# A hybrid decoder layer on one core: more steps between the attention's loads, rotation and parts, and one between store and load of the recurrence's inverses

## The chip, the core and the metric

The kernel runs on one core of a Trainium2 chip. The metric is the device time of one execution in microseconds; the median of several runs is given. The engines are named as in the profile: PE (TensorE; PEld is its weight load), DVE (VectorE), ACT (ScalarE), POOL (GpSimd) and SP (SyncE, which only issues DMAs here). Each engine works off its own queue in order.

## What is computed

One layer on 2048 tokens of width 1024, with 16 learned meta tokens ahead of them. Two mixers run side by side on one input projection, and a gated feed-forward follows:

```python
u = rms_norm(h, norm_mix_g)
proj = u @ w_in + b_in                       # attention | RWKV | two gates
q, k = partial_rope(q, pos), partial_rope(k, pos)
y_attn = sliding_window_sink_attention(q, k, v, sinks)   # window 128, 8 heads, 2 kv heads
y_rwkv = rwkv7_time_mix(p_rwkv, ...)                     # delta-rule recurrence, 8 heads of 64
merged = gates[..., :D] * (y_attn @ w_br_attn) + gates[..., D:] * (y_rwkv @ w_br_rwkv)
h = h + merged @ w_o
f = rms_norm(h, norm_ffn_g)
h = h + (silu(f @ w_gate) * (f @ w_up)) @ w_down
return rms_norm(h, norm_final_g)[:, 16:]
```

## The kernel before

The dense work goes over four blocks of 512 tokens, in two phases: `phase_a(b)` makes the input projection of block b in 37 chunks of 128 columns (`pi`, eight groups of three matmuls each), for b = 0 to 3; then `phase_c(b)` merges the branches (`pb`, `ph_o`), and does the feed-forward (`pg`, `pu`, `ph_d`), for b = 0 to 3. Projections go to DRAM (`proj_d`), the mixers' outputs too (`y_d`), and phase c of a block loads that block's `y_d` (`yl`, split into `ya`).

The mixers are generators that are ticked between the dense matmuls. A `yield` ends a step. Each dense group of three matmuls yields a credit of 0.65, and for each 4.0 / 3 of credit `tick` runs one of three turns; an attention unit moves on in every third turn, so by one step for each 4 of credit, some six dense groups. The recurrence's units (`rwkv(i, j)`, 33 of them, one for each pair of heads and 256 tokens) move in the other two turns, each by one step per three turns, and a new one starts 14 steps after the youngest. Attention units (`attn(ti)`, 16 of 128 tokens each) follow one another: when the last step of one is done, the next starts in the same turn. All the mixers' matmuls stand in TensorE's queue between the dense ones in the order in which the program writes them (`InOrder`). On the other engines a scheduler with a timeline of its own places the instructions, the dense work's with a higher priority.

One attention unit: loads of `cs`, `q`, `qr` (the rotated halves), `kl`, `kr`, `vt`; a step; rotation on GpSimd (L945 to L947, and `roped`, L894 to L896); `set_keys` (`kw`, L884 and L885: each a rounded part and its rest); `parts(0)` (the query's rounded part `qs`, L955 on ScalarE, and its rest, L956 on VectorE); two steps; then for each of two key heads the scores `psS`, the softmax, and the products `py`. After the last `py` ScalarE copies it into `q` (L1014), whose tile has one buffer, and stores it into `y_d` (L1015).

One unit of the recurrence solves 16 triangular blocks on GpSimd (L772 and L774), waits `WAIT_INV` steps, stores the inverses (`xt_d`, L799), loads them again in another layout into the one tile `td` (L804), a step, transposes them on VectorE (L808), a step, `pq` on TensorE, a step, and then four rounds of three steps with the `ch` matmuls, one of which reads `td`. Three more steps, and `pyt` transposes the unit's output, which goes through L869 to L871 into `y_d` (L872).

Of the kernel before, what the change touches and what calls it, by code (L numbers as in the profile page):

```python
# [78 lines left out]
def layer(ctx, tc, x, meta, w_in, w_br, w_o, w_gate, w_up, w_down, w2a, a2, g2, vecs, sinks, gfin,  # L79
# [38 lines left out]
    def f32(ap):  # L118
        return ap.bitcast(F32)
# [497 lines left out]
    def rwkv(i, j):  # L617
# [179 lines left out]
        for _ in range(WAIT_INV):  # L797
            yield
        G.dma_start(xt_d[uid].rearrange("m (b c) i -> b m (c i)", c=4), xv.rearrange("p c i -> p (c i)"))  # L799
        lo, hi = [slice(64 * h, 64 * h + 32) for h in range(2)], [slice(64 * h + 32, 64 * h + 64) for h in range(2)]  # L800
        for h in range(2):
            for q, r32 in ((0, lo[h]), (1, hi[h])):
# [77 lines left out]
    def set_keys(k, cols):  # L880
        for g in range(2):
            gb = slice(64 * g, 64 * g + 64)
            for d in (gb, slice(64 - 64 * g, 128 - 64 * g)):
                A.activation(kw[d, g, 0, cols], k[gb], AF.Copy)  # L884
                V.tensor_sub(kw[d, g, 1, cols], k[gb], f32(kw[gb, g, 0, cols]))  # L885
# [6 lines left out]
    def roped(o, src, rot, cs, w, name):  # L892

        G.tensor_mul(src, src, cs[:, 0])  # L894
        G.tensor_mul(rot, rot, cs[:, 1])
        G.tensor_add(o, src, rot)  # L896
# [28 lines left out]
    def attn(ti):  # L925
# [14 lines left out]
        load_rot(kr, 4, 1, c0, P)  # L940
        vt = mx.tile([P, P], F32, tag="vl", bufs=1, name=f"vl_{ti}")
        S.dma_start(vt, proj_d[5][:, c0:c0 + P])
        yield
        b4 = lambda k: cs[:, k].unsqueeze(1).to_broadcast([P, 4, P])
        G.tensor_mul(q, q, b4(0))  # L945
        G.tensor_mul(qr, qr, b4(1))
        G.tensor_add(q, q, qr)  # L947
        roped(kl[:, 0], kl[:, 0], kr[:, 0], cs, P, ti)
        set_keys(kl[:, 0], own)

        def parts(g):
# [75 lines left out]
    def tick():  # L1027

        turn[0] = (turn[0] + 1) % TURNS
        rs = [u for u in units if u[2] == "r"]  # L1030
        for u in list(units):
            if turn[0] != (0 if u[2] == "a" else 1 if len(rs) > 1 and u is rs[0] else 2):
                continue
            u[1] += 1
            if next(u[0], 0) == 0:
                units.remove(u)
        if todo_r and turn[0] == 2:
            i, j = todo_r[0]
            b = (i or 0) // 2
            young = min((u[1] for u in units if u[2] == "r"), default=LAG)  # L1040
            if young >= LAG - 3 and i not in asked and set(range(6, 9)) <= emitted[b]:
                asked.add(i)
                start("l", lora(i), b)
            if young >= LAG and i in loras and set(
                    range(9, 21) if i is None else range(PAIR0 + 3 * j, PAIR0 + 3 * j + 3)) <= emitted[b]:
                todo_r.pop(0)
                start("r", rwkv(i, j), b)
        if todo_a and turn[0] == 0 and not any(u[2] == "a" for u in units):
            ti = todo_a[0]
            b = (ti or 0) // 4  # L1050
            if set(range(6)) <= emitted[b]:
                todo_a.pop(0)
                start("a", attn_meta() if ti is None else attn(ti), b)
# [135 lines left out]
```

## Time and profile before

| | |
|---|---|
| median of 3 runs | 3375.84 us (3372.03 to 3376.8) |
| profiled execution, its own time | 3377.94 us |
| its span, first to last instruction | 3376.0 us |
| mean granted TensorE clock | 0.987 of full speed |
| busy: PE / PEld / DVE / ACT / POOL | 96% / 79% / 46% / 34% / 34% |
| first and last score matmul `psS` | 142.6 and 1692.0 us |

The span is what the rows below tell of; the execution's own time has 1.9 us around it. Busy shares are means over stages with different limits, so the waits say more than they do. A row of waits reads: who waited, for whom, us in total, times, longest. A row of the timeline reads: start, length, engine, line, what it writes and reads; in brackets how long its engine stood idle before it and who ended that.

### The profile page before, as it was taken

The page shows a single profiled execution, that of the slowest core. Times are in us where ns is not written, and L with a number is a line of the kernel's source. Part 1 is how long each engine was busy: PE and PEld are TensorE (multiplying, and loading weights), DVE is VectorE, ACT ScalarE, POOL GpSimd, SP SyncE. Part 2 cuts the span into 40 slices and gives each one's busy share as a digit, 9 for nine tenths or more (in the row PEclk, how much of TensorE's full clock was granted, in tenths as well). Part 3 has the DMA queues.
Part 4 walks back from the last instruction along what each step waited for, and adds up shares of the span by engine and source line. Part 5 has one row for each costly group of instructions (what it writes and reads, how often), then busy time and mean ns, then how long its engine had stood idle before and what let it go on. Part 6 is the DMA issues. An engine that isn't in the chain of part 4 may idle for free.

```text
span 3376.0 us, 47237 instructions
## 1 busy us (share of the span) xinstructions
PE 3256.3 (96%) x16909; PEld 2681.2 (79%) x16909; DVE 1542.1 (46%) x3622; ACT 1163.2 (34%) x2863; POOL 1156.1 (34%) x2771
## 2 busy tenths in 40 slices
PE   7899999999999998999999999999999999999998
PEld 6777887787888777887787788887888888778887
DVE  3343233232332585666666644445654443542233
ACT  4354344443443455445443422233242221220001
POOL 1124434334344454554453433444333341000000
PEclk9999999999999999999999999999999999999999
DMA  7777666676666776666668555556755555855555
GB/s 262 273 261 241 209 226 211 190 227 197 223 210 215 242 260 206 234 235 234 231 237 280 176 170 174 179 181 201 263 171 177 171 177 176 288 179 191 196 191 181
DMA packets 229448, 721.46 MB, mean 214 GB/s; under 512 B 36333, under 2 KB 90989, under 8 KB 168286
## 3 DMA queue, kind: packets, MB, share of 16 engines
q1 hardware_dynamic: 158126, 516.15, 47.1%
q0 software_dynamic: 38736, 154.99, 12.9%
q10 hardware_dynamic: 32352, 47.31, 3.8%
q8 instruction: 133, 2.18, 0.3%
q14 instruction: 101, 0.83, 0.1%
HBM read 533.46 MB, written 184.82 MB: 213 GB/s over the span
## 4 chain that ended last, share of the span: by engine, by line
PE 60%; DMA 6%; DVE 3%; POOL 3%; ACT 2%; issue 2%; SPq 0%; POOLq 0%; DVEq 0%; ACTq 0%
PE pg L93 14%; PE pu L93 12%; PE ph_d L93 11%; PE pi L93 6%; PE pb L93 4%; PE ch L93 4%; PE ph_o L93 3%; DMA yl<-y_d 1%; PE ph_o_l L93 1%; POOL pr L772 1%; POOL xv L774 1%; DMA lt<-lt_d 1%; PE py L93 1%; PE pq L93 1%; DVE h L202 1%
## 5 line engine op out<-in xcount | busy, mean ns | idle before, releaser
L93 PE MATMUL pi<-act_u,w_in 128*128 128x512 f32 x3552 | 902.5, 402 | 10.5 <-DVE m L202 6.1
L93 PEld LDWEIGHTS pi<-act_u,w_in 128*128 128x128 f32 x3552 | 652.9, 191 | 144.0 <-issue 5.5
L93 PE MATMUL pg<-act_f,w_g 128*128 128x512 f32 x2112 | 533.7, 399 | 6.8 <-DVE act_f L202 6.8
L93 PE MATMUL pu<-act_f,w_u 128*128 128x512 f32 x2112 | 522.9, 395 | 0.0
L93 PE MATMUL ph_d<-w_d,mg_g 128*128 128x512 f32 x1920 | 472.5, 397 | 10.4 <-DVE h L202 10.0
L93 PEld LDWEIGHTS pg<-act_f,w_g 128*128 128x128 f32 x2112 | 388.4, 189 | 85.3 <-DVE act_f L202 9.0
L93 PEld LDWEIGHTS pu<-act_f,w_u 128*128 128x128 f32 x2112 | 388.9, 188 | 78.8 <-issue 1.0
L93 PEld LDWEIGHTS ph_d<-w_d,mg_g 128*128 128x128 f32 x1920 | 355.5, 189 | 85.9 <-DVE h L202 14.5
L772 POOL TENSOR_TENSOR pr<-xv,lt 128x124 f32<-128x124 f32 (+30 forms) x992 | 330.5, 333 | 248.9 <-DMA lt<-lt_d 176.8
L774 POOL TENSOR_TENSOR xv<-xv,pr 128x124 f32<-128x124 f32 (+30 forms) x992 | 341.1, 344 | 74.5
L202 DVE SCALAR_TENSOR_TENSOR h<-ph_d,h 128x512 f32<-128x512 f32 x320 | 218.9, 689 | 130.0 <-PE ph_d L93 128.3
L93 PE MATMUL pb<-ya,w_br 128*128 128x512 f32 x768 | 191.0, 400 | 1.0 <-DMA w_br<-wd_br 0.6
L93 PEld LDWEIGHTS pb<-ya,w_br 128*128 128x128 f32 x768 | 143.1, 191 | 30.9 <-DVE mg_m L202 1.0
L202 DVE SCALAR_TENSOR_TENSOR th<-th,pg 128x512 f32<-128x512 f32 x88 | 60.4, 687 | 214.6 <-ACT th L202 214.5
L93 PE MATMUL ph_o<-w_o,mg_m 128*128 128x512 f32 x576 | 144.2, 400 | 6.8 <-DVE h L202 3.8
L804 POOL DMA_DIRECT2D td<-xt_d x132 | 72.6, 557 | 225.4 <-PE ch L93 197.3
L202 ACT ACTIVATE th<-pg 128x512 f32<-128x512 f32 x88 | 52.6, 598 | 281.4 <-PE pg L93 281.0
L202 DVE TENSOR_TENSOR th<-th,pu 128x512 f32<-128x512 f32 x88 | 60.5, 687 | 183.8 <-PE pu L93 183.3
L243 POOL TENSOR_TENSOR ss_o<-ss_o,mhalf 128x1 f32<-128x1 f32 x16 | 9.4, 590 | 372.5 <-DVE ss_o L202 372.3
L755 POOL DMA_DIRECT2D lt_d<-g x128 | 71.2, 561 | 184.0 <-DVE g L750 182.0
L202 ACT ACTIVATE mg_g<-th 128x512 fp32r<-128x512 f32 x88 | 55.3, 628 | 222.6 <-DVE th L202 222.5
L93 PEld LDWEIGHTS ph_o<-w_o,mg_m 128*128 128x128 f32 x576 | 106.5, 190 | 31.3 <-DVE h L202 5.2
(356 smaller groups left out, 4512.1 us busy)
## 6 DMA issues: line engine op xcount, KB each, us to landing
w_in<-wd_in SPq DMA_DIRECT2D x111, 1024.0 KB, 5.5
w_g<-wd_g SPq DMA_DIRECT2D x66, 1024.0 KB, 5.0
w_u<-wd_u SPq DMA_DIRECT2D x66, 1024.0 KB, 5.0
w_d<-wd_d SPq DMA_DIRECT2D x60, 1024.0 KB, 5.0
wd_in<-w_in POOLq DMA_DIRECT2D x37, 1024.0 KB, 5.8
w_br<-wd_br SPq DMA_DIRECT2D x24, 1024.0 KB, 7.0
wd_g<-w_g POOLq DMA_DIRECT2D x22, 1024.0 KB, 5.2
wd_u<-w_u POOLq DMA_DIRECT2D x22, 1024.0 KB, 5.3
```

Of the source, the lines that this page charges most:

```text
L93: r = f(*p, **k)
L202: return f(*p, **k)
L243: G.tensor_tensor(ss[:rows, 3:4], ss[:rows, 2:3], mhalf[:rows, 0:1], op=ALU.pow)
L755: G.dma_start(lt_d[uid, m0:m0 + n].rearrange("c j i -> j c i"), g[r32, :, 0, o])
L772: G.tensor_mul(pr[:, :, :n_], xv[:, :, r:r + 1].to_broadcast([P, 4, n_]), lt[:, r, r + 1:].unsqueeze(1).to_broadcast([P, 4, n_]))
L774: G.tensor_add(xv[:, :, r + 1:], xv[:, :, r + 1:], pr[:, :, :n_])
L804: G.dma_start(td[r32, :, r32], xt_d[uid, m0:m0 + 4].rearrange("m j i -> j m i"))
```

## The change

Three places get more `yield`s: one after the store of the inverses, one more between the attention's loads and its rotation, and two between the rotation and `set_keys`. An attention unit has three steps more, a unit of the recurrence one more. No other line changes; lines behind these move by 1 to 4.

```diff
@@ -797,6 +797,7 @@
         for _ in range(WAIT_INV):
             yield
         G.dma_start(xt_d[uid].rearrange("m (b c) i -> b m (c i)", c=4), xv.rearrange("p c i -> p (c i)"))
+        yield
         lo, hi = [slice(64 * h, 64 * h + 32) for h in range(2)], [slice(64 * h + 32, 64 * h + 64) for h in range(2)]
         for h in range(2):
             for q, r32 in ((0, lo[h]), (1, hi[h])):
@@ -940,12 +941,15 @@
         load_rot(kr, 4, 1, c0, P)
         vt = mx.tile([P, P], F32, tag="vl", bufs=1, name=f"vl_{ti}")
         S.dma_start(vt, proj_d[5][:, c0:c0 + P])
-        yield
+        for _ in range(2):
+            yield
         b4 = lambda k: cs[:, k].unsqueeze(1).to_broadcast([P, 4, P])
         G.tensor_mul(q, q, b4(0))
         G.tensor_mul(qr, qr, b4(1))
         G.tensor_add(q, q, qr)
         roped(kl[:, 0], kl[:, 0], kr[:, 0], cs, P, ti)
+        for _ in range(2):
+            yield
         set_keys(kl[:, 0], own)
 
         def parts(g):
```

TensorE's queue between attention units 5 and 6: the last `py_5` with the dense product after it, and the first `psS_6`. `pi_2_16` is the projection's chunk 16 in block 2, in the order of the queue 17, 18 and so on follow; a row with x3 is one dense group. Before:

```order
L93 MATMUL py_5_6420<-ptm_5_1_6688,vm_t_129 128x512
L93 MATMUL pi_2_16_6728<-act_u2_7_5697,w_in_2_16_6726 128x512 x3
L93 MATMUL pi_2_17_6813<-act_u2_0_5560,w_in_2_17_6811 128x512 x3
...
L93 MATMUL pi_2_18_6882<-act_u2_7_5697,w_in_2_18_6880 128x512 x3
L93 MATMUL pi_2_19_7059<-act_u2_0_5560,w_in_2_19_7057 128x512 x3
L93 MATMUL pv_6_7063<-cst_80,vl_6_6803 128x128
L93 MATMUL psS_6_0_0_7069<-kw_126,qs_6_0_6865 128x272 x2
```

And now:

```order
L93 MATMUL py_5_7223<-ptm_5_1_7642,vm_t_129 128x512
L93 MATMUL pi_2_30_7707<-act_u2_5_5568,w_in_2_30_7705 128x512 x3
L93 MATMUL pi_2_30_7707<-act_u2_6_5579,w_in_2_30_7705 128x512 x3
...
L93 MATMUL pi_2_35_7958<-act_u2_0_5439,w_in_2_35_7956 128x512 x3
L93 MATMUL pi_2_35_7958<-act_u2_1_5452,w_in_2_35_7956 128x512 x3
L93 MATMUL pv_6_7965<-cst_80,vl_6_7758 128x128
L93 MATMUL psS_6_0_0_7971<-kw_126,qs_6_0_7889 128x272 x2
```

Between the two stand 18 dense groups before and 37 now; both pieces have moved to later chunks, since units 0 to 5 have three steps more each.

GpSimd's queue behind the solve of the recurrence's unit 1_0, where a rotation follows (unit 6's before, unit 5's now; `kr` and `kl` are the keys, `q` the queries). Before:

```order
L774 TENSOR_TENSOR xv_1_0_6163<-xv_1_0_6163,pr_1_0_30_6255 128x4
L799 DMA xt_d_79<-xv_1_0_6163 8x16x128
L768 DMA xv_1_1_6929<-in_consts 128x128
L804 DMA td_118<-xt_d_79 32x4x32 x4
L895 TENSOR_TENSOR kr_6_6797<-kr_6_6797,cs_6_6787 128x128
L896 TENSOR_TENSOR kl_6_6796<-kl_6_6796,kr_6_6797 128x128
L861 TENSOR_TENSOR gst_0_3_6817<-gst_0_3_6817,mhalf_92 128x4
L945 TENSOR_TENSOR q_6_6789<-q_6_6789,cs_6_6787 128x512
L947 TENSOR_TENSOR q_6_6789<-q_6_6789,qr_6_6790 128x512
```

And now:

```order
L774 TENSOR_TENSOR xv_1_0_6012<-xv_1_0_6012,pr_1_0_30_6104 128x4
L799 DMA xt_d_79<-xv_1_0_6012 8x16x128
L768 DMA xv_1_1_6750<-in_consts 128x128
L896 TENSOR_TENSOR kr_5_6558<-kr_5_6558,cs_5_6548 128x128
L897 TENSOR_TENSOR kl_5_6557<-kl_5_6557,kr_5_6558 128x128
L947 TENSOR_TENSOR q_5_6550<-q_5_6550,cs_5_6548 128x512
L949 TENSOR_TENSOR q_5_6550<-q_5_6550,qr_5_6551 128x512
L805 DMA td_118<-xt_d_79 32x4x32 x4
```

The loads of `td` stand behind the rotation here, no longer ahead of it, and the rotation comes right after the store.

TensorE's queue at the end of phase c of block 2, where the last unit of the recurrence transposes its output (`pyt_7_3`); 15 dense groups stand between `pyt_7_3` and block 3's first `pb_3_0_0` before. Before:

```order
L93 MATMUL ph_d2_l_0_0_28174<-w_d2_l_0_28172,mg_g2_20_28022 128x512 x3
L93 MATMUL pyt_7_3_28178<-cst_80,yt_7_3_27733 128x128 x2
L93 MATMUL ph_d2_l_0_0_28174<-w_d2_l_0_28172,mg_g2_21_28099 128x512 x3
L93 MATMUL ph_d2_l_0_1_28195<-w_d2_l_1_28193,mg_g2_20_28022 128x512 x3
L93 MATMUL ph_d2_l_0_1_28195<-w_d2_l_1_28193,mg_g2_21_28099 128x512 x3
L93 MATMUL ph_d2_l_1_0_28213<-w_d2_l_0_28172,mg_g2_20_28022 128x512 x3
```

And now:

```order
L93 MATMUL ph_d2_l_0_1_28187<-w_d2_l_1_28185,mg_g2_20_28014 128x512 x3
L93 MATMUL ph_d2_l_0_1_28187<-w_d2_l_1_28185,mg_g2_21_28089 128x512 x3
L93 MATMUL ph_d2_l_1_0_28205<-w_d2_l_0_28172,mg_g2_20_28014 128x512 x3
L93 MATMUL ph_d2_l_1_0_28205<-w_d2_l_0_28172,mg_g2_21_28089 128x512 x3
L93 MATMUL ph_d2_l_1_1_28216<-w_d2_l_1_28185,mg_g2_20_28014 128x512 x3
L93 MATMUL pyt_7_3_28220<-cst_80,yt_7_3_27754 128x128 x2
```

`pyt_7_3` has moved back by six dense groups; nine are left between it and block 3.

## Rows read from the trace of the kernel before

**Rows 1.** The page: busy us, share, instructions; the clock in 40 slices.

```profile
PE 3256.3 (96%) x16909; PEld 2681.2 (79%) x16909; DVE 1542.1 (46%) x3622; ACT 1163.2 (34%) x2863; POOL 1156.1 (34%) x2771
...
PEclk9999999999999999999999999999999999999999
```

**Rows 2.** Waits of TensorE, whole span: total us, times, longest.

```profile
PE psS L93 <- DVE qs L956: 27.3, 9, 5.8
...
PE ph_d L93 <- DVE h L202: 10.0, 7, 4.5
...
PE pq L93 <- DVE tq L808: 6.9, 2, 5.2
```

**Rows 3.** Groups by line, the scores: busy, mean ns, idle before, releasers.

```profile
L93 PE MATMUL psS<-kw,qs 128*128 128x272 f32 (+1 forms) x256 | 53.2, 332 | 36.1 <-DVE qs L956 27.3 <-ACT kw L884 7.1 <-ACT sig L674 0.9
```

**Rows 4.** Timeline, all engines, 612 to 639 us: one wait of the scores.

```profile
615.12 0.60 ACT L1014 ACTIVATE q<-py 128x512 f32<-128x512 f32 x1 [2.14 <-PE py L93]
...
618.45 0.37 SPq L935 DMA_DIRECT2D q<-proj_d  x1
...
623.45 1.55 POOL L945 TENSOR_TENSOR q<-q,cs 128x512 f32<-128x512 f32 x1 [13.21 <-DMA q<-proj_d]
...
630.13 0.62 ACT L955 ACTIVATE qs<-q 64x512 fp32r<-64x512 f32 x1
...
633.64 0.30 DVE L808 STREAM_TRANSPOSE tq<-td 32x128 f32<-32x128 f32 x1 [3.40 <-DMA td<-xt_d]
...
636.31 0.69 DVE L956 TENSOR_TENSOR qs<-q,qs 64x512 fp32r<-64x512 f32 x1
...
637.05 1.27 PE L93 MATMUL psS<-kw,qs 128*128 128x272 f32 x4 [5.79 <-DVE qs L956]
```

**Rows 5.** Windows at half clock behind score waits, 1 of 7, and their sum.

```profile
634.70:641.50 6.80, 4.45 (x12) 3.71 (x13) 4.41 (x17) 0.00 (x0) 2.30 (x2) 0.50 0.40 147
...
sum 37.40, PE 26.35 PEld 22.56 DVE 16.63 ACT 10.35 POOL 17.64; mean PE 3.76 PEld 3.22 DVE 2.38 ACT 1.48 POOL 2.52
```

**Rows 6.** Windows at half clock behind `ph_d` and `pq` waits: first, sum of 4.

```profile
1542.60:1546.10 3.50, 3.30 (x9) 2.64 (x10) 3.50 (x8) 0.33 (x1) 3.50 (x6) 0.51 0.70 274
...
sum 17.30, PE 15.20 PEld 12.18 DVE 13.54 ACT 2.23 POOL 6.07; mean PE 3.80 PEld 3.05 DVE 3.39 ACT 0.56 POOL 1.52
```

**Rows 7.** Waits of the other engines, whole span.

```profile
POOL td L804 <- PE ch L93: 197.3, 25, 17.7
...
POOL q L945 <- DMA q<-proj_d: 54.9, 8, 13.2
ACT qs L955 <- POOL q L947: 53.0, 13, 10.9
...
DVE qs L956 <- ACT qs L955: 51.7, 10, 12.9
```

**Rows 8.** Timeline, 1536 to 1543 us: a hold on VectorE reaches TensorE.

```profile
1537.92 0.69 DVE L956 TENSOR_TENSOR qs<-q,qs 64x512 fp32r<-64x512 f32 x1 [4.91 <-ACT qs L955]
...
1542.80 0.80 PE L93 MATMUL ph_d<-w_d,mg_g 128*128 128x512 f32 x1 [4.52 <-DVE h L202]
```

**Rows 9.** Timeline, 2894 to 2937 us: last recurrence unit, start of block 3's phase c.

```profile
2895.10 0.38 PE L93 MATMUL pyt<-cst,yt 128*128 128x128 f32 x2
...
2897.79 0.61 POOL L872 DMA_DIRECT2D y_d<-tl  x1 [14.18 <-DVE tl L871]
...
2906.03 0.63 ACT L202 ACTIVATE ya<-yl 128x512 fp32r<-128x512 f32 x1 [4.10 <-DMA yl<-y_d]
...
2906.69 0.69 DVE L202 TENSOR_TENSOR ya<-yl,ya 128x512 fp32r<-128x512 f32 x1 [2.97 <-ACT ya L202]
...
2908.79 8.44 PE L93 MATMUL pb<-ya,w_br 128*128 128x512 f32 x36 [0.36 <-DVE h L202]
...
2936.74 0.50 PE L93 MATMUL ph_o<-w_o,mg_m 128*128 128x512 f32 x1 [3.33 <-DVE h L202]
```

**Rows 10.** Waits of TensorE, 1230 to 1292 us: first merge and normalisation.

```profile
PE ph_o L93 <- DVE mt L202: 3.1, 2, 2.8
```

## The prediction

> **What bounds the kernel now.** I read the busy shares first [rows 1]: TensorE's matmul row is busy 3256.3 of 3376.0 us and no other engine comes near, so the time is TensorE's own work plus the stretches in which it stands still (about 120 us) plus what a lowered clock costs. The clock row shows nines throughout; the mean granted clock is 0.987. Only edits that change TensorE's waits can move the time, so the next view is who ended them [rows 2]. The attention's score product `psS` waits on the second half of its split queries (`qs`, L956), longest 5.8 us; with its other releasers, among them one wait of 7.1 us on the keys `kw`, the score product stands for 36.1 us [rows 3]. The other causes near the change are `ph_d` waiting for VectorE to empty its PSUM tile (10.0) and the inverse's `pq` (6.9).
>
> Next, one such wait in order of time [rows 4]. The last product `py` of one attention unit ends, ScalarE copies it out of PSUM at 615.12 into `q`, and a store sends it away. Since `q` has one buffer, the next unit's load of `q` is issued only at 618.45; GpSimd, idle 13.21 us for it, starts the rotation at 623.45; ScalarE's half of the split follows at 630.13; VectorE's half runs at 636.31, behind a transpose (L808) that waited 3.40 us for a DMA. `psS` starts at 637.05 after 5.79 us of standing. So the chain took 21.9 us from 615.12, and TensorE had 16.1 us of other work to cover it (637.05 - 5.79 - 615.12).
>
> **Added: three steps in front of the score product.** TensorE runs in program order, so the cover can be counted in its rows: between the last `py` of a unit and the first `psS` of the next stand 18 or 19 dense groups of three matmuls before, and 36 or 37 after (31 in the last unit), in all 15 pairs of units. The first fence shows one pair: three products on before, five on after. A group costs 3 x 8.44 / 36 = 0.70 us [rows 9], so 19 more groups are 13.3 us of added cover, mixer work not counted; 12 more, in the last unit, are 8.4 us. The longest wait is 7.1 us. Nor does the chain slip by the same amount: in the order of after, ScalarE's `qs` row still stands about one product behind `py`, as before, because the scheduler places it when its own timeline has the data, and GpSimd's rotation still follows the inverse's store closely (second fence). All these waits should go; I leave 2 us for a late queue: **-34** (bounds -36.1, and -18 if half the units still wait).
>
> **The clock behind these waits.** [...] With the waits go the falls; I take **-12.5** (bounds -13.2 and -6). [...]
>
> **Added: one step between store and load of the inverses.** What the loads of `td` (L804) wait for is mostly not the store: of 33 units 25 wait for the matmul `ch` that last reads `td`, 197.3 us in all on GpSimd [rows 7]. That matmul, the loads, the transpose and `pq` all move by the same step, so the chain to `pq` is neither longer nor better covered. The two `pq` waits, 6.9 us together [rows 2], are thus not what the step is long for; a step later they fall beside other work of VectorE, and I count half of them gone: **-3** (bounds 0, and -12 with the half-clock work that follows them, all but the first row's of [rows 6]).
>
> **The end of the mixers.** The same step moves the last unit's `pyt` six groups later (third fence), 6 x 0.70 = 4.2 us. The last store of `y_d` waits for it and block 3's last `ya` for that store: today `pyt` at 2895.10, store at 2897.79, split ready at 2907.38, while its user, the fourth group of the product that starts at 2908.79, comes at 2910.9 [rows 9]. Cover of 3.5 us is gone and 0.7 us open; the chain now passes more rows of VectorE and GpSimd. The later 3.33 us wait of `ph_o`, on the load of `h`, may absorb some. **+2** (bounds -0.6 and +5).
>
> **Attention that lasts longer.** 16 units of three more steps run past the end of block 0's second phase: `py_15` stood before that block's successor began and stands 324 rows behind it now. At the normalisation that had attention beside it the merge's product waited 3.1 us for VectorE [rows 10]; I charge the second one the same, **+3** (0 to +7). The added steps put no instruction on any engine, and block 1 needs only units 4 to 7, done over a thousand rows earlier.
>
> **Not priced: holds on other engines.** ScalarE idles 53.0 us at `qs` for the rotation and VectorE 51.7 us behind it [rows 7]. These rows keep their places, so the holds stay. One of them reached TensorE: VectorE, 4.91 us in wait at L956, emptied `ph_d` late, and TensorE stood 4.52 us [rows 8]. All `ph_d` waits together are 10.0 us [rows 2], and such ones can vanish or come anew; I take 0 (bounds -10 and +10).
>
> Sum: -34 - 12.5 - 3 + 2 + 3 = **-44.5**. The profiled execution took 3377.94 us (span 3376.0 and 1.9 around it), so 3333.4; it lies 2.1 above the median of the three runs, so I predict **3331 us** against 3375.84.
>
> **Rivals.** (1) The wait survives in part: in the order of after, the loads of `td` stand shortly ahead of the rotation in units 3, 10 and 12, and they can hold GpSimd up to 17.7 us [rows 7]. 21.9 + 17.7 = 39.6 us against a cover of 16.1 + 13.3 = 29.4 leaves 10.2 us, with 2 for the clock, in three units: +36, so 3367. For it: such a hold sat inside the wait shown. Against: the 21.9 already contain a wait of GpSimd, and the longest hold never met the rotation.
>
> (2) The holds move, and it gets slower: TensorE, no longer stopped at `psS`, arrives earlier at dense tiles that VectorE has not emptied. In the input projection three tiles of 24 matmuls cover that (3 x 24 x 0.234 = 16.8 us, over the longest hold, 12.9); in the feed-forward the `ph_d` tiles have 6 matmuls each, 4.2 us for three. Seven units (9 to 15) run there after the change. The one seen cost 4.52 + 1.65 (half of the 3.30 us that TensorE worked at half clock, [rows 6]) = 6.2 us. It decides at 44.5 / 7 = 6.4 us a unit: near that the time is unchanged, 3376; at 9 us it is 63 us against the 44.5, 3331 + 63 = 3394. Against: six units ran there before too, and [rows 2] give `ph_d` 10.0 us in all.
>
> (3) The second part does what it says after all: the transposes stop waiting for `td`, VectorE holds nothing else up, and the `pq` and `ph_d` waits go with their clock, 15.2 / 2 = 7.6 us [rows 6]. 6.9 + 10.0 + 7.6 less the 3 already counted is 21.5: 3310. Against: the 25 waits for `ch` above.
>
> **How the numbers follow.** Forecast, 3316 to 3356: 0.65. Rival 1, to 3369: 0.13. Rival 3, below 3316: 0.05. Rival 2 near its point: 0.10, above it: 0.07. A difference under 0.2% (6.8 us) is about what measurement of this kernel cannot tell from none. Faster 0.83, same 0.10, slower 0.07. The range 3308 to 3366 leaves out most of rival 2 and the end of rival 1.
>
> **What would show it.** `psS` at most 5 us in TensorE's waits; a mean clock of about 0.990 or more; VectorE's and ScalarE's waits at `qs` still near 50 us; the last `psS` past 1850 us instead of 1692; GpSimd's `td` waits on `ch` near 200 us; one wait of a few us at the start of the last block. The prediction is wrong if `psS` still stands for over 15 us, or if `ph_d`, `h` or `pg` gain what it loses.

## The result and the profile after

The changed kernel takes 3340.09 us in the median of three runs (3336.55 to 3347.81) against 3375.84: 0.9898 of the time before, 95% interval 0.9873 to 0.9923. A second series gave 0.9897 (0.9875 to 0.9919). So it gains 1.0%, some 35 us, of the 44.5 that were predicted; the median lies 9 us above the forecast and inside its range.

The profiled execution of after took 3347.81 us, span 3346.0. Of the profile's page, the busy times and the clock in 40 slices, as in [rows 1]:

```profile
PE 3248.2 (97%) x16909; PEld 2677.9 (80%) x16909; DVE 1554.7 (46%) x3622; ACT 1165.7 (35%) x2863; POOL 1158.7 (35%) x2771
...
PEclk9999999999999999999999999999999999999999
```

Span less busy time is how long TensorE stood: 119.7 us before, 97.8 now, 21.9 less. The busy time itself fell by 8.1 us with the same 16909 matmuls, while the time at half clock, told below, fell too; I put it down to the clock. Together they are the 30.0 us of the two spans. The group of the scores, which in [rows 3] had 36.1 us of idle time before it:

```profile
L93 PE MATMUL psS<-kw,qs 128*128 128x272 f32 (+1 forms) x256 | 51.6, 323 | 4.9 <-ACT vz L968 4.9
```

One wait is left, and it is for neither the queries nor the keys. The last `psS` starts at 1931.6 us, past the 1850 that were forecast, and the mean clock is 0.989 (0.991 in the two other runs). TensorE's waits over the whole span (total us, times, longest), as in [rows 2]:

```profile
PE ch L93 <- ACT rd L836: 7.0, 5, 2.6
PE ph_d L93 <- DVE h L202: 6.9, 7, 2.1
...
PE psS L93 <- ACT vz L968: 4.9, 1, 4.9
PE ph_d_l L93 <- DVE h L202: 4.8, 4, 3.1
PE ch L93 <- ACT yt L848: 4.5, 4, 3.3
PE pp L93 <- ACT sig L674: 4.3, 2, 2.9
...
PE pb L93 <- ACT ya L202: 4.2, 1, 4.2
...
PE ch L93 <- DVE ud L841: 3.6, 2, 3.2
...
PE pq L93 <- DVE tq L809: 2.7, 2, 1.4
```

`psS` has lost 31.2 us, `pq` 4.2 and `ph_d` 3.1. Against that the recurrence's product `ch`, which stood 3.7 us before, all of it behind `yt`, stands 15.1 (7.0 + 4.5 + 3.6), and `pp`, which had no wait, 4.3. These two give back 15.7 us, half of what `psS` gave up. The same view of the other engines, answering to [rows 7], and VectorE's wait at the transposes of `td`, which was 19.2 us in 13 waits:

```profile
POOL td L805 <- PE ch L93: 325.3, 27, 27.5
...
ACT qs L959 <- POOL q L949: 47.3, 13, 8.4
...
DVE qs L960 <- ACT qs L959: 44.0, 12, 10.8
POOL q L947 <- DMA q<-proj_d: 42.7, 6, 12.2
```

```profile
DVE tq L809 <- DMA td<-xt_d: 2.6, 5, 1.0
```

ScalarE and VectorE stand at `qs` nearly as long as before, as forecast. But GpSimd stands at the loads of `td` 128 us longer, and VectorE no longer waits for them, which was not.

The windows in which the granted clock was 0.50 or 0.51 of full speed, called half clock here; columns: window, length, then busy time of PE, PEld, DVE, ACT and POOL, clock, DMA share, GB/s. Of seven stretches behind a score wait [rows 5] one is left, the first row; the second row sums all 14 stretches of after:

```profile
261.50:268.40 6.90, 6.28 (x16) 5.02 (x17) 4.93 (x16) 4.73 (x12) 5.87 (x16) 0.51 0.96 326
...
sum 70.70, PE 57.33 PEld 46.45 DVE 42.57 ACT 40.08 POOL 27.27; mean PE 4.09 PEld 3.32 DVE 3.04 ACT 2.86 POOL 1.95
```

Before, the same sum over its 20 stretches was 89.2 us with 70.33 us of TensorE's work. Half the difference in work is 6.5 us. That half is an estimate from the granted 0.50. The matmuls of the projection `pi` come near it: eight took 3.38 us in the window of [rows 5] from 634.70 at 0.50, and 26 took 6.38 us from 641.50 to 650.00 at 1.00, so 0.42 us each against 0.25.

### The profile page after: what moved, and what is told of

It reads as the page before. It is cut to its first block, busy times and chain, and to the rows that moved or that the text cites. A ratio compares the mean times of both kernels' runs of the same rounds, so it can differ in the third digit from the quotient of the medians.

```text
span 3346.0 us, 47222 instructions
## 1 busy us (share of the span) xinstructions
PE 3248.2 (97%) x16909; PEld 2677.9 (80%) x16909; DVE 1554.7 (46%) x3622; ACT 1165.7 (35%) x2863; POOL 1158.7 (35%) x2771
## 4 chain that ended last, share of the span: by engine, by line
PE 74%; DMA 10%; POOL 6%; DVE 4%; ACT 3%; issue 2%; SPq 0%; ACTq 0%; POOLq 0%; DVEq 0%
PE pi L93 18%; PE pg L93 14%; PE pu L93 12%; PE ph_d L93 11%; PE ch L93 4%; PE pb L93 3%; PE ph_o L93 3%; POOL pr L772 2%; POOL xv L774 2%; DMA lt<-lt_d 2%; DMA wr_in<-in_w_in 2%; PE py L93 1%; DMA wr_g<-in_w_gate 1%; PE pq L93 1%; DMA tg<-gate_d 1%
## 5 line engine op out<-in xcount | busy, mean ns | idle before, releaser
L805 POOL DMA_DIRECT2D td<-xt_d x132 | 72.7, 557 | 331.9 <-PE ch L93 325.3
L841 DVE TENSOR_SCALAR ud<-ch,rnb 128x128 f32<-128x128 f32 x128 | 44.6, 348 | 188.6 <-PE ch L93 188.3
L848 ACT ACTIVATE yt<-ch 64x128 f32<-64x128 f32 x128 | 34.9, 273 | 274.4 <-DVE sd L846 273.7
```

The source lines that it names most:

```text
L805: G.dma_start(td[r32, :, r32], xt_d[uid, m0:m0 + 4].rearrange("m j i -> j m i"))
L841: V.tensor_scalar(ud, un, rnb[:, c:c + 1], None, op0=ALU.mult)
L848: A.activation(yt[64 * (c % 2):64 * (c % 2) + 64, c // 2], see[64:128], AF.Copy)
```

## Experiments

Ratios are to the kernel before on the same chip; "us" is the median of the kernel's own runs. In short:

| edit to the kernel before | us | ratio (95%) | PE stands | of it psS |
|---|---|---|---|---|
| none | 3375.84 | | 119.7 | 36.1 |
| attention's three steps | 3347.27 | 0.9918 (0.9902 to 0.9933) | 94.7 | 6.3 |
| recurrence's step | 3351.93 | 0.9932 (0.9919 to 0.9946) | 98.4 | 21.7 |
| load step alone | 3363.51 | 0.9965 (0.9954 to 0.9977) | 102.9 | 17.6 |
| two steps ahead of the keys | 3345.75 | 0.9910 (0.9897 to 0.9923) | 96.5 | 4.8 |
| recurrence's step ahead of the store | 3351.44 | 0.9927 (0.9909 to 0.9946) | 99.0 | 23.2 |
| recurrence's step ahead of the transposes | 3346.99 | 0.9922 (0.9905 to 0.9939) | 98.7 | 23.2 |
| recurrence's step behind `ch` | 3383.46 | 1.0025 (1.0011 to 1.0039) | 119.7 | 30.3 |
| free `q`, no step | 3356.78 | 0.9952 (0.9935 to 0.9969) | 111.1 | 9.8 |
| six steps in the attention | 3356.95 | 0.9945 (0.9926 to 0.9964) | 105.9 | 0.0 |
| the change (second series) | 3341.80 | 0.9897 (0.9875 to 0.9919) | 100.3 | 5.5 |
| the change and free `q` | 3325.84 | 0.9855 (0.9837 to 0.9874) | 87.0 | 3.6 |
| the same less the load step | 3337.34 | 0.9888 (0.9867 to 0.9909) | 94.1 | 0.9 |

The column "PE stands" is span less PE's busy time, and the column beside it is a part of it, in us. Both are of one profiled execution, which can lie off the median of its row: by 9.7 us above it with free `q`, by 7.1 above it for the change, by 4.5 below it with the step behind `ch`, by 3.8 below it for the change and free `q`. The kernel with the step ahead of the transposes computes something else, as told there.

**The attention's three steps alone**, the two lower places of the diff.

> The attention's three steps without the recurrence's step. Theory (the gain is the cover in front of the score product, 36 or 37 dense groups as in the changed kernel): 3343 us (3335 to 3352), psS at most 6 us in TensorE's waits, pq still near 7 us, VectorE's tq waits on the load of td still near 19 us. Rival (the recurrence's step carries part of the gain through holds on VectorE): 3352 to 3362 us, with psS gone but ph_d and pq at 15 us or more together.

3347.27 us, 0.9918. `psS` 6.3 (0.3 over the theory's 6), `pq` 6.8, VectorE's wait at the transposes 17.8: the theory. The rival's sign is absent (`ph_d` and `pq` 14.2 us together, under its 15, and the time under its range). `ch` stands 12.0 us here already, but not for the same instructions: 0.1 of it behind `rd`, which is 7.0 of the 15.1 with the whole change, and 6.5 behind VectorE's `ud`.

**The recurrence's step alone**, the first place of the diff.

> The recurrence's step without the attention's. The cover in front of psS stays at 18 or 19 groups. Theory (the transposes move with their loads, so nothing is covered better): 3373 us (3366 to 3380), psS near 36 us. Rival (the step lets VectorE pass the transposes without a wait; one such wait of 3.40 us lay inside the psS wait shown of before): VectorE's tq waits on the load of td fall from 19.2 to about 3 us, psS loses 5 to 12 us, 3352 to 3364 us.

3351.93 us, 0.9932: the theory is wrong and the rival right, with a little more gained than it said (`psS` loses 14.4 us, not 5 to 12). Waits of this kernel by TensorE, and by GpSimd and VectorE around the recurrence's small loads:

```profile
PE psS L93 <- DVE qs L957: 14.9, 8, 4.0
...
PE pq L93 <- DVE tq L809: 2.1, 2, 2.0
```

```profile
POOL td L805 <- PE ch L93: 285.5, 25, 25.8
...
POOL lt_d L755 <- DVE g L750: 87.0, 25, 14.3
```

```profile
DVE tq L809 <- DMA td<-xt_d: 1.9, 4, 0.7
```

By the separate ratios the two parts are worth 27.7 us (0.0082 x 3375.84) and 23.0, 50.7 in sum; together they gained 34.4. They are two cures for largely the same waits: of the 36.1 us at `psS`, the recurrence's step takes 14.4, which the attention's steps take as well. What the recurrence's step adds on top of the attention's is not clear of noise: 0.9897 (0.9875 to 0.9919) with both, 0.9918 (0.9902 to 0.9933) with the attention's alone.

**One part of the attention's steps at a time.** First the load step:

```diff
-        yield
+        for _ in range(2):
+            yield
         b4 = lambda k: cs[:, k].unsqueeze(1).to_broadcast([P, 4, P])
```

> One more step between loads and rotation alone: 24 or 25 dense groups in front of psS, about 6 more, 4.2 us. Theory (each wait shrinks by the cover): the eleven psS waits of before, each less 4.2 us, leave about 7 us (2.9 + 0.5 + 1.6 + 1.5 + 0.4); with most of the clock back 3345 us (3338 to 3354). Rival (the rotation slips with its step, so cover ahead of it doesn't count): psS 25 us or more, 3362 to 3376 us.

3363.51 us, 0.9965: the time lies in the rival's range, but `psS` with 17.6 us lies between the two. Its group shows why:

```profile
L93 PE MATMUL psS<-kw,qs 128*128 128x272 f32 (+1 forms) x256 | 52.1, 324 | 17.6 <-ACT sig L674 7.1 <-ACT bt_None L783 3.9 <-ACT kw L884 2.9
```

The split queries, 27.3 us before, are down to one wait of 0.7, and the keys to 2.9 (7.1 less the 4.2 of cover). For these two the theory held. TensorE's busy time did not fall with it (3257.9 us against 3256.3), so none of the clock came back (mean 0.987 in both). What stands there instead is ScalarE emptying PSUM tiles of the recurrence, as here in the timeline:

```profile
237.89 0.63 ACT L202 ACTIVATE w_in<-wr_in 128x512 fp32r<-128x512 f32 x1 [1.06 <-DMA wr_in<-in_w_in]
...
238.82 0.57 ACT L783 ACTIVATE bt_None<-pb_None 128x512 f32<-128x512 f32 x1
...
239.45 0.82 PE L93 MATMUL psS<-kw,qs 128*128 128x272 f32 x2 [3.88 <-ACT bt_None L783]
```

A later `psS` needs a PSUM tile; the one it gets is emptied by `bt_None`, and that stands in ScalarE's queue behind the conversion of weights that a DMA delivers late.

Then the two steps ahead of `set_keys`:

> The two steps between rotation and set_keys alone: 30 or 31 dense groups in front of psS, 12 more, 8.4 us, over the longest wait of 7.1 us. Theory: psS at most 4 us, 3343 us (3335 to 3352), so the third step adds nothing. Rival (a queue in front of the rotation is late by more than one wait, so each step counts): psS 8 to 15 us, 3350 to 3362 us.

3345.75 us, 0.9910 (0.9897 to 0.9923), `psS` 4.8 (0.8 over the theory's 4): as all three steps. The third gives nothing that these runs can tell, as long as `q` is loaded late. Nor can they tell this kernel, two `yield`s in all, from the whole change at 0.9897.

**Where the recurrence's step must stand.** Three kernels with one `yield` each, at other places of the unit. Ahead of the store:

```diff
+        yield
         G.dma_start(xt_d[uid].rearrange("m (b c) i -> b m (c i)", c=4), xv.rearrange("p c i -> p (c i)"))
```

> The kernel before with the recurrence's step placed ahead of the store of the inverses, so that store, load and transpose keep their distances and only stand a step later among everything else. Theory (what gained 24 us with the step behind the store is that the loads of td have landed when VectorE comes to the transposes): VectorE's tq waits on the load stay near 19 us, psS 28 us or more, 3372 us (3364 to 3382). Rival (any step gains, by shifting the recurrence against the attention): 3352 us (3344 to 3360), psS near 22 us.

3351.44 us, 0.9927, transposes' wait 2.0, `psS` 23.2: the same gain. So the gain does not need the step to stand between store and load. But the wait of the transposes fell with it, against the theory, so this kernel does not rule that wait out as the cause. Behind the loads:

```diff
+        yield
         tq = mx.tile([P, n, 32], F32, tag="tl", bufs=2, name=f"tq_{nm}")
```

> The kernel before with the recurrence's step between the loads of td and the transposes. Theory (as for the step ahead of the store: VectorE must find td landed): tq waits under 4 us, psS near 22 us, pq near 2 us, 3352 us (3344 to 3361). Rival (it is GpSimd's queue that gained, the loads no longer standing right behind the store): tq waits under 4 us as well, but psS 28 us or more and 3364 us or more.

In this kernel the last of a unit's four reads of `td` falls behind the next unit's load and takes that unit's inverses, so it computes something else; its load also no longer waits for that read (23.4 us of waits on `ch` in place of 197.3). 3346.99 us, 0.9922, `psS` 23.2, `pq` 0.2. These are the theory's numbers, and no wait of the transposes for `td` is left. With `td` landed far ahead the gain is no larger. Behind the last round of `ch`:

```diff
         if m:
             return
+        yield
 
         y4 = yt.rearrange("p t (h v) -> p (t h) v", v=64)
```

> The kernel before with the recurrence's step behind its last round of ch, ahead of the unit's own output work: loads, transposes, pq and ch keep their places among the other units' work, and a unit is one step longer all the same. Theory now (the step gains because the loads of td, their transposes and pq come a step later against the next unit's early work, which holds GpSimd and VectorE): no gain, tq waits near 19 us, psS 30 us or more, 3370 us (3362 to 3380). Rival (any extra step of the recurrence gains, since it thins its work out): 3352 us (3344 to 3360), psS near 22 us.

3383.46 us, 1.0025 (1.0011 to 1.0039): no gain, rather a loss of 0.25%. Its waits at the three places:

```profile
PE psS L93 <- DVE qs L957: 23.1, 7, 7.2
...
PE pq L93 <- DVE tq L808: 8.0, 2, 5.2
```

```profile
DVE tq L808 <- DMA td<-xt_d: 11.2, 12, 2.4
```

```profile
POOL lt_d L755 <- DVE g L750: 181.8, 30, 22.1
```

The unit is as long as in the three kernels with the step ahead of `pq`, only `td`, `tq`, `pq` and `ch` have their old places. A unit of the recurrence starts 14 steps after the last one, so a step ahead of `pq` moves these against the next unit's early work, and a step behind them doesn't. These kernels show where the step must stand: ahead of `pq` it gains, behind `ch` it doesn't, so a longer unit by itself is not what gains. Why is not settled by them, since the three that gain have more in common than that distance: each also has one step more between a unit's own solve and its `pq`. The same step with the next unit started 15 steps after the last would keep the old distance and leave the longer way to `pq`, and so tell the two apart; it was not run.

Two waits go with the gain. GpSimd's wait for VectorE's `g` (L750, the matrices of the next unit's solve, stored by L755) is 182.0 us before and 181.8 with the step behind `ch`; it is 87.0, 89.4 and 124.8 with it behind the store, ahead of the store and ahead of the transposes. VectorE's wait at the transposes is 19.2 before, 11.2 with the step behind `ch`, and 2.0 or less in the other three. How long GpSimd stands in all is no sign of a gain: with the step behind the store its wait at the loads of `td` grew by 88.2 us while the one for `g` fell by 95.0.

**How that reaches the scores** is seen at one place, attention unit 7 (counted from 0), which has the third longest wait of before (5.67 us). Kernel before, timeline:

```profile
809.80 0.42 DVE L750 TENSOR_TENSOR g<-pg,rnb 128x256 f32<-128x256 f32 x1
...
810.52 2.25 POOL L755 DMA_DIRECT2D lt_d<-g  x4 [1.72 <-DVE g L750]
...
817.29 1.02 PE L93 MATMUL py<-ptm,vm_t 128*128 128x512 f32 x2
...
828.33 0.40 POOL L772 TENSOR_TENSOR pr<-xv,lt 128x124 f32<-128x124 f32 x1 [8.78 <-DMA lt<-lt_d]
...
834.97 1.26 POOL L945 TENSOR_TENSOR q<-q,cs 128x512 f32<-128x512 f32 x1
...
838.45 0.69 DVE L956 TENSOR_TENSOR qs<-q,qs 64x512 fp32r<-64x512 f32 x1 [12.88 <-ACT qs L955]
...
839.19 1.05 PE L93 MATMUL psS<-kw,qs 128*128 128x272 f32 x3 [5.67 <-DVE qs L956]
```

The same unit with the recurrence's step alone:

```profile
789.38 0.42 DVE L750 TENSOR_TENSOR g<-pg,rnb 128x256 f32<-128x256 f32 x1 [2.82 <-PE pg L93]
...
790.22 2.25 POOL L755 DMA_DIRECT2D lt_d<-g  x4
...
799.56 1.02 PE L93 MATMUL py<-ptm,vm_t 128*128 128x512 f32 x2
...
804.41 0.40 POOL L772 TENSOR_TENSOR pr<-xv,lt 128x124 f32<-128x124 f32 x1 [6.22 <-DMA lt<-lt_d]
...
812.80 1.30 POOL L946 TENSOR_TENSOR q<-q,cs 128x512 f32<-128x512 f32 x1
...
817.78 0.74 PE L93 MATMUL psS<-kw,qs 128*128 128x272 f32 x4 [2.46 <-DVE qs L957]
```

Here `q` had long been loaded: its rotation has no idle time before it. It stood in GpSimd's queue inside a solve (13 rows of `pr` and `xv` are ahead of it in the first kernel, 18 in the second), and the solve waited for `lt`. Counted from the last `py`, `g` comes 7.5 us ahead in the first and 10.2 in the second, the solve starts 11.0 and 4.8 us behind, the rotation 17.7 and 13.2. In the first kernel VectorE came to `g` late (no idle time before it), in the second it stood ready and waited 2.82 us for TensorE. This is one unit, at which it is a solve's `g` that comes earlier; that the other score waits shrink for the same reason was not traced one by one.

**A free `q`.** The unit's output goes into the tile of the last transposed scores, so that the next unit's load waits for no store:

```diff
-        A.activation(q, py.rearrange("p (j t) -> p j t", t=P), AF.Copy)
-        A.dma_start(y_d[0:4, :, ti * P:(ti + 1) * P].rearrange("f p t -> p f t"), q)
+        yo = mx.tile([P, 4, P], F32, tag="pt", bufs=1, name=f"yo_{ti}")
+        A.activation(yo, py.rearrange("p (j t) -> p j t", t=P), AF.Copy)
+        A.dma_start(y_d[0:4, :, ti * P:(ti + 1) * P].rearrange("f p t -> p f t"), yo)
```

> The kernel before, with the unit's output written into the tile of the last transposed scores (pt) and not into q, so that the next unit's load of q waits for no store; no step is added, 18 or 19 groups stay in front of psS. Theory (the chain begins with the load that waits for the unit before): the chain is some 5 us shorter, psS 5 to 12 us, 3350 us (3340 to 3360). Rival (GpSimd and VectorE are late for the recurrence, not for q): psS 20 us or more, 3362 to 3378 us.

3356.78 us, 0.9952, `psS` 9.8, of which 7.7 are the first unit's keys, which no `q` holds up. The chain told from [rows 4] is right: the waits at `qs` are down from 27.3 us to 2.1. But of 26.3 us at `psS` only 8.6 show in TensorE's standing in its profiled execution (119.7 to 111.1), the slowest of six: `ch` stands 9.9 us, `py` 8.4 and `ph_o_l` 6.7, 6.2, 3.6 and 6.5 more than before. The longest wait of `ch`, 5.5 us at 1360, is behind `rd` on ScalarE, and there ScalarE had waited 12.2 us for a load of weights.

With the change:

> The changed kernel with the same free q. Theory (psS is covered there already, nothing is left to gain at it): as the changed kernel, 3340 us (3332 to 3349). Rival (ScalarE and VectorE stand 47 and 44 us at qs in the changed kernel, and these holds make the new waits of ch, 15 us; with q loaded earlier both shrink): holds under 60 us together, ch under 8 us, 3324 to 3334 us.

3325.84 us, 0.9855 (0.9837 to 0.9874), the fastest kernel of this study; its interval ends where that of the change begins. The rival's numbers came: ScalarE's wait at `qs` for the rotation is 1.7 us in place of 47.3, VectorE's wait at `qs` is

```profile
DVE qs L960 <- ACT qs L959: 24.2, 9, 5.2
```

and `ch` stands 0.7 us in place of 15.1. Nine stretches at half clock are left of 14, 43.1 us in place of 70.7 (mean clock 0.993 in place of 0.989); TensorE's busy time is 15.2 us under that of the change and its standing 10.8, so more than half of what these two profiles differ by is busy time. The rival's mechanism, a hold at `qs` that reaches `ch`, is there at one place of after in the timeline:

```profile
812.27 1.26 POOL L949 TENSOR_TENSOR q<-q,qr 128x512 f32<-128x512 f32 x1
813.56 0.63 ACT L959 ACTIVATE qs<-q 64x512 fp32r<-64x512 f32 x1 [8.37 <-POOL q L949]
814.10 0.43 ACT L836 ACTIVATE rd<-ch 64x64 f32<-64x64 f32 x2
...
814.58 0.79 PE L93 MATMUL ch<-rd,td 128*128 128x128 f32 x2 [2.60 <-ACT rd L836]
```

`rd`, which the next `ch` needs, stands behind `qs` on ScalarE, and `qs` waited 8.37 us for GpSimd; TensorE pays 2.60, and its granted clock, 1.00 from 810 to 814, is 0.50 for the 3.4 us from 814.5.

But the five other waits of `ch` over 1 us in after have no hold at `qs` in front of them. The two longest are 3.17 us behind `ud` at 1235.91 and 3.28 behind `yt` at 1298.72. In the first VectorE stood for GpSimd at a normalisation (`ss_f`):

```profile
1234.71 0.49 DVE L202 TENSOR_SCALAR f<-h,ss_f 128x512 f32<-128x512 f32 x1 [4.52 <-POOL ss_f L243]
...
1235.51 0.35 DVE L841 TENSOR_SCALAR ud<-ch,rnb 128x128 f32<-128x128 f32 x1
```

In the second ScalarE stood for a load of weights:

```profile
1297.73 0.63 ACT L202 ACTIVATE w_u<-wr_u 128x512 fp32r<-128x512 f32 x1 [2.58 <-DMA wr_u<-in_w_up]
...
1298.39 0.27 ACT L848 ACTIVATE yt<-ch 64x128 f32<-64x128 f32 x1
```

The other three, all behind `rd`, had ScalarE waiting for a load of the recurrence's projections (1.47 us at 594.80), for GpSimd's rotated keys (1.22 at 1721.55) and at a normalisation (1.24 at 1870.41). So these six waits of `ch`, 13.0 of the 15.1 us, are holds in the queues of ScalarE and VectorE, 2.60 us of them at `qs`. That a free `q` takes nearly all of them away is shown by this run; why it takes the others, at which ScalarE and VectorE wait for something else than the rotated `q`, is open.

Without the load step:

> The kernel before with the two steps ahead of set_keys, the recurrence's step and the free q, without the further step between loads and rotation. Theory (30 groups cover the shortened chain): as the changed kernel with the free q, 3326 us (3319 to 3333). Rival (that step also keeps ScalarE and VectorE from standing at qs): 3334 to 3345 us, with ch waits back at 7 us or more.

3337.34 us, 0.9888 (0.9867 to 0.9909). The time is in the rival's range and its mechanism is not there: `ch` stands 3.6 us, ScalarE waits 3.6 at `qs`, yet `py` stands 7.8 behind ScalarE's `ptt` (2.3 with the step) and there are 13 stretches at half clock in place of 9 (mean clock 0.990 in place of 0.993). The intervals of this kernel and of the one with the step overlap a little, so that the step gains there is likely and not settled.

**More steps than the chain needs.** Three between loads and rotation, four ahead of `set_keys`, without the recurrence's:

> The kernel before with six more steps in an attention unit in place of three (two between loads and rotation, four ahead of set_keys) and without the recurrence's step: 55 or 56 dense groups in front of psS. Theory (cover beyond the chain's length is worth nothing): as with three steps alone, 3346 us (3338 to 3355), psS at most 6 us. Rival (longer attention units cost by themselves, by running beside more of the dense phases): ph_d, ph_o and ch together 10 us or more above those of three steps (28 us), 3356 to 3370 us.

3356.95 us, 0.9945, against 0.9918 with half as many added. `psS` stands 0.0, so this cover is complete, and the time is no better, by its median worse; the two intervals overlap a little (0.9926 to 0.9964 against 0.9902 to 0.9933), so that worse is likely and not settled. The group of the down projection:

```profile
L93 PE MATMUL ph_d<-w_d,mg_g 128*128 128x512 f32 x1920 | 473.5, 398 | 17.3 <-DVE h L202 16.0 <-ACT sf L837 0.6 <-DVE th L202 0.5
```

It stood 7.4 us with three steps. The last scores now start at 2186.9 us instead of 1927.5, so more units run beside the feed-forward. `ch` fell from 12.0 us to 5.1 and `ph_o` rose from 3.8 to 6.3: the three of them stand 28.7 us against 23.2 with three steps (the 28 us of the expectation count 4.8 of `ph_d_l` too, which is 2.0 here), not the 10 more of the rival. So of the rival's mechanism it is mainly `ph_d` that is there, and the time is at the lower end of the rival's.

**The change once more:**

> The changed kernel itself, beside the others of this call: 0.990 of the kernel before (0.987 to 0.993), 3341 us. If both parts' gains were separate, 0.9932 times 0.9918 would make it 0.985; 0.990 says that they take largely the same waits.

3341.80 us, 0.9897: as forecast.

## Why the prediction was right, and where it was not

**What bounds the kernel, and the cover.** Right. Two steps ahead of the keys take the score waits to 4.8 us and three to 6.3; a load of `q` that waits for no store takes them to 9.8 with no step at all. The term of -34 for `psS` measured -31.2; the 4.9 left are a wait for ScalarE to empty a PSUM tile (`vz`) and not the chain.

**The clock behind it.** Taken as -12.5 for seven stretches at half clock. No run shows this term by itself: that a stretch costs half of the work done in it was my estimate, 13.2 us for the 26.35 in [rows 5]; the `pi` matmuls above, 0.42 us against 0.25, make it somewhat less than half. In its place the runs show this. One of the seven stretches is left, with 6.28 us of work, 3.1 lost by the same estimate: -10.1. But other stretches took their place, and over all of them half of TensorE's work at half clock fell by 6.5 us; its busy time fell by 8.1. What the other 1.6 us come from is not shown. With the change and free `q` the busy time is 23.3 us under that of before, at a mean clock of 0.993 against 0.987.

**The step between store and load.** The amount for `pq` was near (-3 against -4.2), and the reason was wrong. The step that failed is "the chain to `pq` is neither longer nor better covered", from which followed that the transposes would go on waiting and GpSimd's `td` waits stay near 200 us. They are 325.3, VectorE waits 2.6 us instead of 19.2, and alone the step gains 23 us. What I left out is likely the next unit: all these instructions move together, but they move against the work of the unit that starts 14 steps behind, on GpSimd's and VectorE's queues. That this is the cause, and not the step more that a unit's own solve gets ahead of `pq`, no run shows. Rival 3 is right that the transposes stop waiting. Its price (21.5 us more than the 3) is near the 23 of the step alone by luck: it was made of `pq`, `ph_d` and their clock, and of the 16.9 us of these two waits the step alone took 9.9, while 14.4 came off `psS`, which rival 3 does not price. In the change the attention's steps had already taken those, and 3310 did not come.

**The end of the mixers.** +2 was taken; `pb` stands 4.2 us at the start of the last block and `ph_o` no longer waits there for `h`, which with `pb` had been 3.33 + 0.36 us in [rows 9]; behind the new wait follow 3.4 us of work at half clock (0.50 from 2883.0), by the same estimate 1.7 lost, which the old one did not have (1.00 from 2908.8 to 2930). 0.5 + 1.7 is 2.2: right. **Attention that lasts longer**: +3 was taken, and `ph_o` behind `mt` went from 3.1 to 2.4 us, so nothing in sum: the second merge now waits 2.1 us, as charged, and the first only 0.2. With twice the steps the same concern shows at another place, `ph_d`.

**The holds.** This is the term that was mis-sized. I gave it 0 (bounds -10 and +10), and looked for it at `ph_d`. It came at `ch` (+11.4), `pp` (+4.3) and `ph_d_l` (+2.6), with half clock behind some of it (0.50 from 814.5 and from 1299.2); `ph_d` lost 3.1. All waits of TensorE but those at `psS`, `pq`, `pb` and `ph_o`, which other terms price, grew by 13.8 us in sum, over the upper bound. And it is not the hold that I named: ScalarE and VectorE stand 47.3 and 44.0 us at `qs`, as I said they would, and of the new waits of `ch` 2.60 us are behind `qs`.

The profiled execution misses its sum by 14.4 us (3347.81 against 3333.4). Of that about 10.1 is standing (-21.9 against -34 - 3 + 2 + 3 = -32) and 4.4 clock (-8.1 against -12.5). It is also the slowest of its three runs, 7.7 us over the median.

**Rivals 1 and 2.** No score wait behind a late `td` load is left, so rival 1 is out. Rival 2 is out at three steps; at six its wait of `ph_d` is there, 17.3 us, and the gain shrinks without being lost.

## What to carry to other kernels

Added steps paid here until the chain in front of the waiting product was covered (`psS` 36.1 us without, 4.8 with two); beyond that they gained nothing, and at six steps `ph_d` paid for them (17.3 us against 7.4 with three). Before adding cover, look at what makes the chain start late: a buffer that the previous unit's store still holds may share another tile, as here with `pt`; on top of the steps that was worth another 0.4%. When a step moves one unit's instructions, look at what they now meet of the next unit's, and not only at the chain they belong to. Don't add up two parts that cure the same wait. And before a new wait is put down to one hold, look at all the places where it stands: the one that fits may be a small part.

## What was not expected of the hardware

A wait of GpSimd, which is 3% of the chain of work that ended last before the change, grew by 128 us (at the loads of `td`, 197.3 to 325.3) in a kernel that became 1% faster: how long it waits there does not tell what the wait costs. The three kernels with the recurrence's step ahead of `pq` show it: GpSimd stands there 285.5, 286.0 and 23.4 us, and all three take 0.992 to 0.993 of the time before (the last of them computes something else, as told). Whether VectorE waits for a small load was decided by about 1 us: from issue to landing a `td` load takes 3.6 us in the median before the change and 3.8 after it, and VectorE came to the transposes a median 4.0 us after the last issue before the change (over its 64 transposes) and 5.1 after it; that is 19.2 us of waits against 2.6. How much of the time hangs on these waits is not shown: with the step behind `ch` they fell to 11.2 us and nothing was gained.
